# Three steps' weight sums are made early and kept in DRAM, and two more steps of the last round go by sums

## The chip, the cores and the metric

One core of one Trainium2 chip runs the whole kernel. Five engines work side by side, each through its own list of instructions in order: TensorE (PE, with its weight loads as PEld) multiplies, VectorE (DVE) and ScalarE (ACT) do elementwise work, GpSimd (POOL) does a little of it and issues some transfers, SyncE (SP) issues nearly all others. The metric is the time of one execution on the device in microseconds (us), as the median of several runs.

## The reference

The reference is one layer of a streaming encoder for 256 tokens of width 2048, all in float32: a gated linear attention, then an MLP with squared ReLU, each behind an RMSNorm and with a residual, and a last RMSNorm.

```python
h = x
h = h + gla_mixer(rmsnorm(h, gla_norm), w_in, w_gate_up, b_gate, o_norm, w_out)   # q, k, v, r and a gate out of w_in
h = h + (relu(rmsnorm(h, mlp_norm) @ w_up) ** 2) @ w_down                          # 2048 -> 8192 -> 2048
return rmsnorm(h, final_norm)
```

Nearly all time goes into products of the 256 tokens with float32 weights, which come from DRAM once each.

## The kernel before

**Products in parts.** A float32 number is used as the sum of two: `hi`, a rounded copy that ScalarE makes (`copy_hi`), and `lo`, what is left, a subtraction on VectorE. A product is then three matmuls, hi by hi, hi by lo and lo by hi. A weight tile of 512 KB thus goes: SP loads it into a `raw` tile (six of them and one more, in turn), ScalarE makes hi, VectorE makes lo, each into one of five slots (`slots()`), and TensorE multiplies. ScalarE and VectorE run ahead of TensorE by as many steps as there are slots free.

**Products by sums.** For the down product of the MLP (and parts of w_out) a step takes a pair of 128 weight rows by 512 columns, as a 2 by 2 grid of blocks. A plain step is 8 block products of 3 matmuls, 24 in all. A step "by sums" (Strassen's way in Winograd's form) forms sums of the activations' blocks (`form_sums`) and of the weight's blocks (`weight_sums`) and makes 7 block products, 21 matmuls. It costs VectorE and ScalarE more: first hi and lo of three quarters of the raw tile, whose first quarter is meanwhile turned into a sum by an accumulating DMA of POOL, then two instructions of `weight_sums` in place in the raw tile, then hi and lo of the whole tile again (`of_sums`). TensorE correspondingly has two parts, 9 matmuls on the raw tile and later 12 on the sums; they add into four PSUM banks, P16, B32, P57 and BX4.

**The order of the work.** First the mixer: `natural` and `turned` stream the columns of w_in (v, k, q, then the rest of v, then r); small work between steps is queued in `side` and done by `pump`, one item per step. In the order of the trace the second half of v is multiplied from about 140 us (line 554). Then w_out, then the MLP in eight rounds of 1024 hidden units: `up` makes the round's activations, `down` adds the round's part of the result. Up steps run 18 ahead of down steps and interleave with them. `down` goes through passes (m, g), round m and column group g, four steps kp = 0 to 3 each. When the up steps have ended, the last ten down steps run alone: (6, 0) from kp 2, (7, 0) and (7, 1). Column groups 2 and 3 of the last round come after these, as eight plain steps of another shape (line 1229 on), which use two further tiles, `room` and `hf`, in the place of the turned activations `hth` and `htl` (tags Ah and Al).

**What goes by sums.** `by_sums(m, g, kp)` (line 850) says it: all steps of rounds 0 to 5, most of round 6, and in round 7 only (0, 2), (0, 3) and (1, 2), written (g, kp).

**Banks between passes.** When a pass of a new column group begins, the banks of the old group are saved to SBUF and new ones are filled from it, both by ScalarE: `settle(k)` does the saving of bank k (`sums<-acc` or `h<-acc` in the profile), `begin(k, g)` the filling (`acc<-sums` or `acc<-h`). Where they stand among the steps hangs on `first`, the first step of the pass that goes by sums: in a pass that runs alone P16 is saved and filled at `kp == first`, P57 at the step after, B32 and BX4 are saved at that step too (line 1162). All of these copies go through `copy_end`, and a later `copy_hi` is put behind the last of them in ScalarE's list (`last_end`).

Of the kernel before, what the change touches and what calls it, by code (L numbers as in the profile page):

```python
# [46 lines left out]
G = 1024  # L47
GT = 512
# [13 lines left out]
MR = 2 * GT  # L62
ROUNDS = HID // MR
# [5 lines left out]
def tile_gla_mlp(ctx, tc, x, xt, cols, w_vg, w_in, w_gate, w_out, w_up, w_down, final_norm, out):  # L69
    nc = tc.nc  # L70

    const = ctx.enter_context(tc.tile_pool(name="const", bufs=1))
    big = ctx.enter_context(tc.tile_pool(name="big", bufs=2))
# [2 lines left out]
    tmp = ctx.enter_context(tc.tile_pool(name="tmp", bufs=2))  # L76
    st = ctx.enter_context(tc.tile_pool(name="st", bufs=3))
    psum = ctx.enter_context(tc.tile_pool(name="psum", bufs=1, space=bass.MemoryType.PSUM))

    acc_free, aux_free = deque(range(6)), deque([6, 7])  # L80

# [9 lines left out]
        return psum_bank(aux_free[-1], "aux")  # L91


    side = deque()

    def pump(n=1):

        with tc.issue_after(last_hi[0].ins), tc.issue_after(last_lo[0].ins):
            for _ in range(n):
                if side:  # L100
                    side.popleft()()

    def flush():
        while side:
# [5 lines left out]
    last_load, last_hi, last_lo, last_sum, last_end = [None], [None], [None], [None], [None]  # L110
# [9 lines left out]
    def slots():  # L120
        return [wpool.tile([P, SLOT], F32R, tag=i, name=i) for i in ("hi", "lo")]
# [56 lines left out]
    def natural(row, source, n, cuts, pumps=1, ahead=None, order=range(KT)):  # L178

        acc = acc_banks(NT * len(cuts))  # L180
        acc = [acc[t * len(cuts) : (t + 1) * len(cuts)] for t in range(NT)]
        for step, kt in enumerate(order):
            wh, wl = weights(source(kt), n, ahead and ahead(kt))
            terms = lambda t: [(row(kt, t)[x], (wh, wl)[y]) for x, y in ((0, 0), (0, 1), (1, 0))]
            if ahead and step == 0:
                for c, (lo, hi) in enumerate(cuts):
                    for i in (0, 2, 1):
                        for t in range(NT):
                            s, w = terms(t)[i]
# [16 lines left out]
    def turned(row, w, c0, even=(0,), acc=None):  # L206

        acc = acc or acc_banks(GT // P // 2)
        for kp in range(KT // 2):
            wh, wl = pair_of(w, kp, c0, even)  # L210
            for i in range(2):
                kt = 2 * kp + i
                ah, al = row(kt)
                for j in range(GT // P):
                    s = slice(j * P, (j + 1) * P)
                    o = acc[j // 2][:, j % 2 * T : (j % 2 + 1) * T]
                    for n, (u, m) in enumerate(((wh, ah), (wh, al), (wl, ah))):

                        nc.tensor.matmul(  # L219
                            o, u[:, i, s], m, start=kt == 0 and n == 0 and j % 2 == 0,  # L220
                            stop=kt == KT - 1 and n == 2, skip_group_check=True,
                        )
                if kt < KT - 1:
                    pump()
        return acc

    HALF = [(0, 512), (512, 1024)]
# [323 lines left out]
    side.extend([nothing] * 4 + [lambda: two_scores(0), nothing, lambda: two_scores(2)])  # L551


    acc = natural(row_x, rows(w_in, 3 * KEYW), G, HALF, order=even_at(9, 11))
    flush()
    for t in range(NT):
# [46 lines left out]
    def weight_sums(u):  # L603
        nc.vector.tensor_tensor(u[:, 2], u[:, 0], u[:, 2], op=ALU.subtract)  # L604
        return nc.vector.tensor_tensor(u[:, 1::2], u[:, 1::2], u[:, 2:3].to_broadcast([P, 2, T]), op=ALU.subtract)  # L605

    FORMED = (0, 1, 7)
    in_forms = lambda a: a.rearrange("p (f s) -> p f s", f=8)
# [241 lines left out]
    def by_sums(m, g, kp):  # L850

        if m == ROUNDS - 1:
            return (g, kp) in ((0, 2), (0, 3), (1, 2))
        return m < ROUNDS - 2 or g != order_of(m)[-1] or kp == 1


# [174 lines left out]
    def down(passes):  # L1031
# [3 lines left out]

        ahead = pending = None
        quick = False
        units = 0
        for n, (m, g) in enumerate(passes):
            fresh = not n or passes[n - 1][1] != g  # L1040
# [11 lines left out]
            for kp in range(KP):  # L1052
                last = ends and kp == KP - 1
                alone = units + LEAD >= UPS
                by_parts = by_sums(m, g, kp)

                def products(n, these, w, banks=banks, last=last):

# [11 lines left out]
                raw = raw_tile()[:, : 2 * GT]  # L1070
                c0 = m * MR + 2 * kp * P
                src = w_down[c0 : c0 + 2 * P, g * GT : (g + 1) * GT].rearrange("(i p) c -> p i c", p=P)
                if by_parts:
                    for i in range(2):
                        last_load[0] = nc.sync.dma_start(out=raw[:, i * GT : (i + 1) * GT], in_=src[:, i])

                    nc.gpsimd.dma_start(out=raw[:, :T], in_=src[:, 0, T:], accum_op=ALU.add)  # L1077
                else:
                    last_load[0] = nc.sync.dma_start(out=raw.rearrange("p (i c) -> p i c", i=2), in_=src)
# [13 lines left out]
                if by_parts:  # L1093
                    these = (P16, 0, at(A11), block(1)), (B32, T, at(A12), block(3)), (B32, 0, at(S4), block(2))
                    u = raw.rearrange("p (f s) -> p f s", f=4)

                    with tc.issue_after(last_lo[0].ins):
                        last_sum[0] = weight_sums(u).ins
                else:
                    these = [  # L1100
                        (k, 0, at(f[i]), block(2 * i, 2))
                        for i in range(2) for k, f in ((B32, (A11, A12)), (BX4, (A21, A22)))
                    ]
# [10 lines left out]

                ahead_of = passes[n + 1] if last and n + 1 < len(passes) else None

                def of_sums(u=raw, products=products, at=at, kp=kp, banks=banks, quick=fresh and quick, g=g, then=ahead_of):


                    nonlocal ahead  # L1120
                    to = slots()

                    if quick and kp < 2:
                        settle((B32, P16)[kp])
                        if kp == 0:
                            banks[P57] = begin(P57, g)
                    if then and by_sums(*then, 0):
                        ahead = {k: begin(k, then[1]) for k in (B32, P16)}
                    for a in range(2):
                        copy_hi(*(x.rearrange("p (f s) -> p f s", f=4)[:, a::2] for x in (to[0][:, :G], u)))  # L1130
                    if quick and kp == 0:
                        settle(P57)
                        banks[BX4] = begin(BX4, g)
                    elif quick and kp == 1:
                        settle(BX4)
                    with tc.issue_after(last_lo[0].ins):
                        last_lo[0] = nc.vector.tensor_tensor(to[1][:, :G], u, to[0][:, :G].bitcast(F32), op=ALU.subtract)  # L1137
                    early = (P57, 0, at(S1), block(0)), (P16, T, at(S2), block(2))
                    late = (P57, T, at(S3), block(1)), (BX4, T, at(A22), block(3))
                    products(0, early, to)  # L1140
                    yield
                    products(0, late, to)
                    products(1, (*early, *late), to)

                if by_parts:
                    if alone:

                        pending = of_sums()
                    else:
                        rest = of_sums()  # L1150
                        next(rest)
# [167 lines left out]
```

## Time and profile before

| | us |
|---|---|
| median of 3 runs (lowest to highest) | 1044.37 (1044.07 to 1044.48) |
| the profiled execution, its own time | 1043.33 |
| its span, first to last instruction | 1041.5 |
| busy in the span: TensorE, VectorE, ScalarE, POOL | 1033.2, 865.3, 736.9, 119.5 |
| share of the chain of waits that is TensorE's | 99% |

A row of a group shows line, engine, operation, output and inputs, shape and count, then busy time in us, mean time of one in ns, and the engine's idle time before it with what ended most of it. A row of the timeline shows start and duration in us, then the same, and in brackets the idle time before and its releaser; equal instructions in a row are merged (x8). Times of the timeline count from the start of the span. A row of the stretches shows a window, its length, the busy time of each engine (PE, PEld, DVE, ACT, POOL) with the number of instructions, the granted clock, the busy share of the DMA engines and what they moved in GB/s. A row of the issues shows the transfer, the engine whose queue it is, the count, the size of one and the median time in us from issue to landing. TensorE's matmuls overlap, so the steps between starts tell its pace, not the durations.

### The profile page before, as it was taken

What the parts mean: (1) busy time and instruction counts of PE and PEld (TensorE: products, weight loads), DVE (VectorE), ACT (ScalarE), POOL (GpSimd) and SP (SyncE); (2) the same over time, 40 slices, a digit from 0 to 9 for tenths busy, and PEclk for the clock granted to TensorE, in tenths of its full rate; (3) what the DMA queues carried; (4) which work ended last, traced back from release to release, by engine and by line L of the source; (5) the groups of instructions that cost most, each with busy time, mean ns of one, the idle gap of its engine ahead of it and who ended that gap; (6) DMA issues with size and microseconds to landing.
All of it is one profiled execution on the core that took longest, in us unless ns stands there. A gap on an engine that the chain in (4) does not pass through costs nothing.

```text
span 1041.5 us, 23180 instructions
## 1 busy us (share of the span) xinstructions
PE 1033.2 (99%) x9058; PEld 1032.8 (99%) x9058; DVE 865.3 (83%) x1171; ACT 736.9 (71%) x1088; POOL 119.5 (11%) x163
## 2 busy tenths in 40 slices
PE   9999999999999999999999999999999999999997
PEld 9999999999999999999999999999999999999997
DVE  6668654657599876989999999999999999999887
ACT  7685544546477665677778788778778778778685
POOL 0000000010111101111111121111111121111100
PEclk9999999999999999999999999999999999999999
DMA  9957664655667687678887887887888888887772
GB/s 341 338 164 220 189 199 144 181 145 180 194 182 210 206 263 197 175 207 239 224 249 226 230 233 227 233 243 214 253 227 225 245 228 228 237 233 219 234 243 86
DMA packets 119453, 226.79 MB, mean 218 GB/s; under 512 B 10752, under 2 KB 27904, under 8 KB 119216
## 3 DMA queue, kind: packets, MB, share of 16 engines
q1 hardware_dynamic: 100768, 207.46, 63.2%
q0 software_dynamic: 17856, 16.26, 10.3%
q10 hardware_dynamic: 720, 1.60, 0.4%
q8 instruction: 71, 1.16, 0.4%
q14 instruction: 38, 0.31, 0.1%
HBM read 223.17 MB, written 2.10 MB: 216 GB/s over the span
## 4 chain that ended last, share of the span: by engine, by line
PE 99%; issue 0%; ACT 0%; DVE 0%; POOLq 0%; POOL 0%; DVEq 0%
PE up L867 33%; PE acc L867 28%; PE acc L176 19%; PE acc L725 8%; PE acc L219 6%; PE aux L219 2%; PE aux L176 1%; PE aux L627 1%; PE aux L523 1%; PE aux L252 0%; ACT sqf L1206 0%; PE acc L424 0%; DVE hf L1278 0%; POOLq L1315 0%; POOL rf L358 0%
## 5 line engine op out<-in xcount | busy, mean ns | idle before, releaser
L118 ACT CAST hi<-raw 128x512 fp32r<-128x512 f32 (+4 forms) x634 | 512.0, 834 | 234.8 <-PE acc L176 69.0
L131 DVE TENSOR_TENSOR lo<-raw,hi 128x768 fp32r<-128x768 f32 (+3 forms) x226 | 238.0, 1057 | 100.1 <-ACT hi L118 97.4
L867 PE MATMUL acc<-hi,act 128*128 128x256 f32 x1696 | 247.7, 276 | 0.0
L867 PE MATMUL up<-hh,hi 128*128 128x256 f32 x1024 | 238.7, 276 | 0.0
L867 PE MATMUL up<-hl,hi 128*128 128x256 f32 x1024 | 238.7, 276 | 0.0
L165 DVE TENSOR_TENSOR lo<-raw,hi 128x1024 fp32r<-128x1024 f32 x160 | 194.7, 1219 | 28.3 <-ACT hi L118 26.3
L867 PEld LDWEIGHTS acc<-hi,act 128*128 128x128 f32 x1696 | 217.6, 188 | 0.0
L867 PEld LDWEIGHTS up<-hl,hi 128*128 128x128 f32 x1024 | 192.2, 188 | 0.0
L867 PEld LDWEIGHTS up<-hh,hi 128*128 128x128 f32 x1024 | 192.2, 188 | 0.0
L1077 POOL DMA_DIRECT2D raw<-in_w_down x112 | 97.1, 867 | 516.1 <-DMA raw<-in_w_down 231.0
L1137 DVE TENSOR_TENSOR lo<-raw,hi 128x1024 fp32r<-128x1024 f32 x112 | 136.4, 1218 | 1.1 <-ACT hi L118 1.1
L867 PE MATMUL up<-hh,lo 128*128 128x256 f32 x1024 | 137.0, 276 | 0.0
L867 PE MATMUL acc<-lo,act 128*128 128x256 f32 x848 | 133.8, 276 | 0.0
L867 PEld LDWEIGHTS up<-hh,lo 128*128 128x128 f32 x1024 | 125.7, 188 | 0.0
L867 PEld LDWEIGHTS acc<-lo,act 128*128 128x128 f32 x848 | 113.4, 188 | 0.0
L176 PE MATMUL acc<-hi,xA 128*128 128x256 f32 (+1 forms) x736 | 105.6, 278 | 0.0
L176 PEld LDWEIGHTS acc<-hi,xA 128*128 128x128 f32 x736 | 94.4, 188 | 0.0
L605 DVE TENSOR_TENSOR raw<-raw 128x512 f32<-128x512 f32 x124 | 85.6, 690 | 3.2
L176 PE MATMUL acc<-lo,xA 128*128 128x256 f32 (+1 forms) x368 | 61.5, 278 | 0.0
L604 DVE TENSOR_TENSOR raw<-raw 128x256 f32<-128x256 f32 x124 | 52.4, 423 | 2.9
L176 PEld LDWEIGHTS acc<-lo,xA 128*128 128x128 f32 x368 | 50.8, 188 | 0.2 <-DVE lo L131 0.2
L219 PE MATMUL acc<-xA,hi 128*128 128x256 f32 x288 | 49.2, 276 | 0.0
(181 smaller groups left out, 1220.0 us busy)
## 6 DMA issues: line engine op xcount, KB each, us to landing
raw<-in_w_up SPq DMA_DIRECT2D x128, 512.0 KB, 4.6
raw<-in_w_down SPq DMA_DIRECT2D x224, 256.0 KB, 4.3
raw<-in_w_in SPq DMA_DIRECT2D x80, 512.0 KB, 3.8
raw<-in_w_down POOLq DMA_DIRECT2D x112, 128.0 KB, 5.0
raw<-in_w_out SPq DMA_DIRECT2D x20, 512.0 KB, 4.9
raw<-in_w_down SPq DMA_DIRECT2D x16, 512.0 KB, 5.0
raw<-in_w_vg SPq DMA_DIRECT2D x14, 520.0 KB, 8.1
raw<-in_w_out SPq DMA_DIRECT2D x24, 256.0 KB, 3.5
```

Source lines behind the costliest of these rows:

```text
L118: last_hi[0] = nc.scalar.copy(to, raw)
L131: last_lo[0] = nc.vector.tensor_tensor(lo[:, s], raw[:, s], hi[:, s].bitcast(F32), op=ALU.subtract)
L165: last_lo[0] = nc.vector.tensor_tensor(to[1], dst, to[0].bitcast(F32), op=ALU.subtract)
L176: nc.tensor.matmul(o[:, m], x, w[:, m], start=first and c == 0, stop=last, skip_group_check=True)
L219: nc.tensor.matmul(o, u[:, i, s], m, start=kt == 0 and n == 0 and j % 2 == 0, stop=kt == KT - 1 and n == 2, skip_group_check=True,)
L523: nc.tensor.matmul(o, kab[:, k[0], c0 + c, k[1] : k[1] + P], q(qt[:, c0 + c]), start=c == 0, stop=c == 1)
L604: nc.vector.tensor_tensor(u[:, 2], u[:, 0], u[:, 2], op=ALU.subtract)
L605: return nc.vector.tensor_tensor(u[:, 1::2], u[:, 1::2], u[:, 2:3].to_broadcast([P, 2, T]), op=ALU.subtract)
L725: newest[0] = nc.tensor.matmul(bank[:, o + d : o + d + T], x, w[:, d : d + T], start=bank in sums_banks and bank.name not in begun, stop=l ...
L867: newest[0] = nc.tensor.matmul(o, x, w, start=first, stop=last, skip_group_check=True).ins
L1077: nc.gpsimd.dma_start(out=raw[:, :T], in_=src[:, 0, T:], accum_op=ALU.add)
L1137: last_lo[0] = nc.vector.tensor_tensor(to[1][:, :G], u, to[0][:, :G].bitcast(F32), op=ALU.subtract)
```

## The change

In the last round five steps instead of three go by sums: (0, 2), (0, 3), (1, 1), (1, 2), (1, 3). The weight sums of the last three, those of pass (7, 1), are no longer made in `down`. They are made in the mixer: `make_sums` loads the weight tile with SP into a raw tile, VectorE forms all sums in it (three instructions), ScalarE and VectorE make hi and lo in a pair of the slots, and two DMAs of POOL store them, 512 KB each, in DRAM tiles. Each of the three tiles is two jobs and an empty one; `pump` does one job per step, so they go with the first nine steps of the second half of v. In the order in which the built kernel's instructions stand, these loads come among that pass's loads in SP's list, and the six stores are next to each other in POOL's list.

In `down` these three steps load three quarters of their raw tile (in two transfers), and hi and lo of the sums (two transfers of 512 KB) into `pre` tiles, which take the place of `hth` and `htl`; SP's list has the sums of kp 3 ahead of those of kp 1 and 2. The accumulating DMA, `weight_sums` and the second hi and lo go away there. TensorE does the 9 matmuls of kp 1, the 9 of kp 2, the 12 of kp 1, the 9 of kp 3 and then the 12 of kp 2 and of kp 3. With (1, 1) by sums `first` of pass (7, 1) is 1 and no longer 2, so that the savings and fillings of the banks stand one step earlier. Before pass (7, 1) TensorE's list is the same in both kernels. The activations of (7, kp 1) now need `form_sums`, and their parts are made over the full width.

```diff
+    dram = ctx.enter_context(tc.tile_pool(name="dram", bufs=1, space=bass.MemoryType.DRAM))
...
-    side = deque()
+    side, jobs = deque(), deque()
...
                 if side:
                     side.popleft()()
+            if jobs:
+                jobs.popleft()()
...
+    MADE_DOWN = ((1, 1), (1, 2), (1, 3))
+    made = {}
+
+    def make_sums(key, src):
+
+        made[key] = dram.tile([2, P, G], F32, tag=f"made{len(made)}", name="made")
+        raw, to = [], []
+
+        def high():
+            raw.append(raw_tile()[:, :G])
+            with tc.issue_after(last_load[0].ins):
+                last_load[0] = nc.sync.dma_start(out=raw[0].rearrange("p (i c) -> p i c", i=2), in_=src)
+            u = raw[0].rearrange("p (f s) -> p f s", f=4)
+            nc.vector.tensor_tensor(u[:, 0], u[:, 0], u[:, 1], op=ALU.add)
+            weight_sums(u)
+            to.extend(slots())
+            nc.scalar.copy(to[0][:, :G], raw[0])
+            nc.gpsimd.dma_start(out=made[key][0], in_=to[0][:, :G].bitcast(F32))
+
+        def low():
+            nc.vector.tensor_tensor(to[1][:, :G], raw[0], to[0][:, :G].bitcast(F32), op=ALU.subtract)
+            nc.gpsimd.dma_start(out=made[key][1], in_=to[1][:, :G].bitcast(F32))
+
+        return high, low
...
+        for high, low in todo:
+            jobs.extend([high, low, lambda: None])
...
+    make_all()
     acc = natural(row_x, rows(w_in, 3 * KEYW), G, HALF, order=even_at(9, 11))
...
         if m == ROUNDS - 1:
-            return (g, kp) in ((0, 2), (0, 3), (1, 2))
+            return (g, kp) in ((0, 2), (0, 3), (1, 1), (1, 2), (1, 3))
...
+                ready = made.get((m, g, kp))
...
-                if by_parts:
+                if ready is not None:
+                    last_load[0] = nc.sync.dma_start(out=raw[:, T:GT], in_=src[:, 0, T:])
+                    last_load[0] = nc.sync.dma_start(out=raw[:, GT:], in_=src[:, 1])
+                    if not rooms:
+                        for i in "hl":
+                            rooms.extend(big.tile([P, 2, 2, G], F32R, tag="A" + i, name="pre", bufs=1).rearrange("p b i c -> b p i c"))
+                    ready_in = rooms.pop(0)
+                    for i in range(2):
+                        last_load[0] = nc.sync.dma_start(out=ready_in[:, i].bitcast(F32), in_=ready[i])
+                    ready = [ready_in[:, i] for i in range(2)]
+                elif by_parts:
...
-                    with tc.issue_after(last_lo[0].ins):
-                        last_sum[0] = weight_sums(u).ins
+                    if not ready:
+                        with tc.issue_after(last_lo[0].ins):
+                            last_sum[0] = weight_sums(u).ins
...
-                    to = slots()
+                    copied = not to
+                    to = to or slots()
...
-                    for a in range(2):
+                    for a in range(2 * copied):
                         copy_hi(*(x.rearrange("p (f s) -> p f s", f=4)[:, a::2] for x in (to[0][:, :G], u)))
...
-                    with tc.issue_after(last_lo[0].ins):
-                        last_lo[0] = nc.vector.tensor_tensor(to[1][:, :G], u, to[0][:, :G].bitcast(F32), op=ALU.subtract)
+                    if copied:
+                        with tc.issue_after(last_lo[0].ins):
+                            last_lo[0] = nc.vector.tensor_tensor(to[1][:, :G], u, to[0][:, :G].bitcast(F32), op=ALU.subtract)
...
                         pending = of_sums()
+                        if last and n + 1 == len(passes):
+                            for _ in pending:
+                                pass
```

More of the change, by code (lines that the diff above doesn't have):

```diff
@@ L225, in turned, with weight_sums, make_all @@
         return acc
+    def weight_sums(u):
+        nc.vector.tensor_tensor(u[:, 2], u[:, 0], u[:, 2], op=ALU.subtract)
+        return nc.vector.tensor_tensor(u[:, 1::2], u[:, 1::2], u[:, 2:3].to_broadcast([P, 2, T]), op=ALU.subtract)
+    MADE_OUT = ()
+    MADE_DOWN = ((1, 1), (1, 2), (1, 3))
[17 more added lines that the diff above has]
+        return high, low
+    def make_all():
+        pair = lambda w, c0, g: w[c0 : c0 + 2 * P, g * GT : (g + 1) * GT].rearrange("(i p) c -> p i c", p=P)
+        todo = [make_sums((None, g, kp), pair(w_out, 2 * kp * P, g)) for g, kp in MADE_OUT]
+        todo += [make_sums((ROUNDS - 1, g, kp), pair(w_down, (ROUNDS - 1) * MR + 2 * kp * P, g)) for g, kp in MADE_DOWN]
+        for high, low in todo:
+            jobs.extend([high, low, lambda: None])
     HALF = [(0, 512), (512, 1024)]
@@ L601, in form_sums @@
         tt(f[:, S4], f[:, A12], f[:, S2], ALU.subtract)
-    def weight_sums(u):
-        nc.vector.tensor_tensor(u[:, 2], u[:, 0], u[:, 2], op=ALU.subtract)
-        return nc.vector.tensor_tensor(u[:, 1::2], u[:, 1::2], u[:, 2:3].to_broadcast([P, 2, T]), op=ALU.subtract)
     FORMED = (0, 1, 7)
@@ L1037, in down @@
         quick = False
+        rooms = []
         units = 0
@@ L1115, in down, with of_sums @@
                 ahead_of = passes[n + 1] if last and n + 1 < len(passes) else None
-                def of_sums(u=raw, products=products, at=at, kp=kp, banks=banks, quick=fresh and quick, g=g, then=ahead_of):
+                def of_sums(u=raw, products=products, at=at, kp=kp, banks=banks, quick=fresh and quick, g=g, then=ahead_of, to=ready):
                     nonlocal ahead
-                    to = slots()
+                    copied = not to
+                    to = to or slots()
                     if quick and kp < 2:
```

## The prediction, made before the changed kernel ran

> **What bounds the kernel now.** I read the page first, then the chain of waits, then the timelines of TensorE, ScalarE, VectorE and SyncE in the two stretches that the change touches.
>
> ```profile
> span 1041.5 us, 23180 instructions
> PE 1033.2 (99%) x9058; PEld 1032.8 (99%) x9058; DVE 865.3 (83%) x1171; ACT 736.9 (71%) x1088; POOL 119.5 (11%) x163
> ...
> GB/s 341 338 164 220 189 199 144 181 145 180 194 182 210 206 263 197 175 207 239 224 249 226 230 233 227 233 243 214 253 227 225 245 228 228 237 233 219 234 243 86
> ...
> PE 99%; issue 0%; ACT 0%; DVE 0%; POOLq 0%; POOL 0%; DVEq 0%
> ```
>
> TensorE is the chain from end to end; the other engines matter only where they make it wait. So a change is worth the matmuls that it removes, less the waits that it adds. The end of the last round, as TensorE runs it:
>
> ```profile
> 1003.15 1.07 PE L867 MATMUL acc<-hi,act 128*128 128x256 f32 x8
> 1004.06 0.62 PE L867 MATMUL acc<-lo,act 128*128 128x256 f32 x4
> 1004.51 1.98 PE L867 MATMUL acc<-hi,act 128*128 128x256 f32 x16
> 1006.32 1.07 PE L867 MATMUL acc<-lo,act 128*128 128x256 f32 x8
> 1007.23 0.84 PE L867 MATMUL acc<-hi,act 128*128 128x256 f32 x6
> 1007.91 0.50 PE L867 MATMUL acc<-lo,act 128*128 128x256 f32 x3
> ...
> 1012.33 0.96 PE L176 MATMUL acc<-hi,act 128*128 128x256 f32 x7
> ```
>
> A plain step is 24 matmuls (16 hi, 8 lo), from 1004.51 to 1007.23: 2.72 us, 0.113 each. A step by sums is 21, in two parts: 9 on the raw tile (1007.23), later 12 on its sums (1003.15 shows the 12 of pass (7,0), kp 3). In 1003.15 to 1012.33 nothing waits.
>
> **The matmuls saved.** In pass (7,1) kp 1 and kp 3 go from 24 to 21: 6 x 0.113 = 0.68 us less. That is all that the change can give TensorE; the order before pass (7,1)'s second step stays the same.
>
> **The new wait at 1004.5.** ScalarE and VectorE in that stretch:
>
> ```profile
> 999.75 2.31 ACT L118 CAST hi<-raw 128x512 fp32r<-128x512 f32 x3
> 1004.48 0.59 ACT L994 COPY sums<-acc 128x512 f32<-128x512 f32 x1 [2.42 <-PE acc L867]
> 1004.96 0.60 ACT L994 COPY acc<-sums 128x512 f32<-128x512 f32 x1
> 1005.48 1.05 ACT L118 CAST hi<-raw 128x1024 fp32r<-128x1024 f32 x1
> ...
> 1009.51 1.08 ACT L994 COPY h<-acc 128x512 f32<-128x512 f32 x2
> 1010.47 1.07 ACT L118 CAST hi<-raw 128x1024 fp32r<-128x1024 f32 x1
> ```
> ```profile
> L118 ACT CAST hi<-raw 128x768 fp32r<-128x768 f32 x124 | 103.1, 832 | 6.5 <-PE up L867 2.1 <-ACT some L780 1.7 <-PE acc L176 1.7
> L131 DVE TENSOR_TENSOR lo<-raw,hi 128x768 fp32r<-128x768 f32 x124 | 118.1, 953 | 25.5 <-ACT hi L118 23.8 <-PE up L867 1.4 <-DMA raw<-in_w_down 0.2
> ```
>
> At 1004.48 ScalarE saves bank P16 of the pass just ended and at 1004.96 fills P16 of pass (7,1); the 2.42 us before are a wait for TensorE's last matmul into the old P16. Now this costs nothing: `settle(P16)` stands at kp 2, behind two casts, and TensorE has 24 plain matmuls to run. In the changed kernel the first step by sums is kp 1, so the pair stands at kp 1, ahead of the cast of kp 2, and TensorE has only kp 1's 9 to run, of which the last 3 write P16. The pair can't start sooner: it waits for the same matmul. Queued behind it on ScalarE: the cast of kp 2, P57's pair, two copies h<-acc (now at kp 2 too), the cast of kp 3. Worked with the rows' durations; release and restart come from the one wait of this kind that the trace has:
>
> ```profile
> 10.19 1.24 DVE L131 TENSOR_TENSOR lo<-raw,hi 128x1040 fp32r<-128x1040 f32 x1 [1.06 <-ACT hi L118]
> ...
> 11.49 0.41 PEld L176 LDWEIGHTS acc<-lo,xA 128*128 128x128 f32 x3 [0.23 <-DVE lo L131]
> 11.49 0.62 PE L176 MATMUL acc<-lo,xA 128*128 128x256 f32 x3
> ```
>
> VectorE ended at 11.43, TensorE started at 11.49: release 0.06. Three matmuls took 0.62 against 0.50 at 1007.91: restart 0.12.
>
> - 1004.51 plus 6 matmuls = 1005.19. P16 is filled at 1005.56, released at 1005.62: wait 0.43.
> - Three matmuls and a restart: 1006.08. Cast of kp 2: 1005.48 + 0.83 = 1006.31, released 1006.37: wait 0.29.
> - Six: 1007.17. VectorE's lo of kp 2: 1006.34 + 0.95 = 1007.29, released 1007.35: wait 0.18.
> - Three, then kp 1's 12 from the stored sums (P57 filled at about 1007.3, in time): 1009.17. The copies h<-acc take ScalarE from 1007.2 to 1008.2, the cast of kp 3 to 1009.0, in time. Six: 1009.85. Lo of kp 3: 1009.03 + 0.95, released 1010.04: wait 0.19.
> - Three, 12 of kp 2, 12 of kp 3: 1013.22.
>
> The 1012.33 row thus moves to 1013.22. Waits 1.09 and four restarts 0.48 make 1.57; less 0.68, that is +0.89 us. Ends: no wait at all, -0.68, if the copies ended sooner than their rows say; or each wait longer by a ScalarE copy of 0.6 that slips ahead, +1.5. I take the replay, since every term has its row a few us away.
>
> The rest runs later by the same 0.9: from 1009.94 ScalarE's casts for the final steps come some 0.5 us sooner than now (1010.47), so nothing more waits there. The output's tail behind the last matmul is not touched.
>
> **The loads of the sums.** They go into the room of the turned activations, free when the last up matmul has run:
>
> ```profile
> 983.77 0.28 PE L867 MATMUL up<-hl,hi 128*128 128x256 f32 x1
> ...
> 984.34 1.07 PE L867 MATMUL up<-hh,lo 128*128 128x256 f32 x8
> ```
> ```profile
> 981.31 0.80 SPq L1075 DMA_DIRECT2D raw<-in_w_down  x2
> 983.07 0.38 SPq L1079 DMA_DIRECT2D raw<-in_w_down  x1
> 988.85 0.81 SPq L1075 DMA_DIRECT2D raw<-in_w_down  x2
> 991.24 0.38 SPq L1079 DMA_DIRECT2D raw<-in_w_down  x1
> 993.36 19.79 SPq L168 DMA_DIRECT2D raw<-in_w_down  x8
> ```
> ```profile
> 983.00:1006.00 23.00, 23.00 (x206) 23.00 (x205) 19.52 (x27) 15.19 (x21) 1.72 (x2) 1.00 0.82 243
> ```
> ```profile
> fb<-in_final_norm ACTq DMA_DIRECT2D x1, 1024.0 KB, 6.7
> ```
>
> SyncE has 12 issues for kp 1 to 3 where it had 4; 8 x 0.40 = 3.2 us of a queue that is mostly free. Kp 3's sums stand first and wait for the lo half's room until 984.1 (SyncE would have issued kp 1's raw at 983.07); kp 1's raw follows at 984.9 instead, kp 1's and kp 2's sums at 985.4 to 987. Behind them stand kp 2's raw (988.85, held by a raw tile anyway), kp 3's, and the final steps' eight. Three MiB of sums come in, 0.5 MiB of raw loads goes: +2.6 MB. Needed first: kp 2's raw at 1005.5, behind 3.75 MiB of SyncE's own and the 1.2 MB that ScalarE's and POOL's queues load there (the gain row above and one sum of 128 KB): 5.1 MB in 21.7 us, 235 GB/s; this stretch moves 243, the page's first slice 341. At 341 it lands 7 us early, so I take 0; the other end is in the rivals.
>
> **VectorE before the end.** Kp 1's activation forms of round 7 now need sums: three more adds and a full-width subtract, where VectorE has no idle time:
>
> ```profile
> 962.92 0.96 DVE L131 TENSOR_TENSOR lo<-raw,hi 128x768 fp32r<-128x768 f32 x1 [0.16 <-ACT hi L118]
> ...
> 972.32 1.22 DVE L1137 TENSOR_TENSOR lo<-raw,hi 128x1024 fp32r<-128x1024 f32 x1
> ```
> ```profile
> 975.08 0.62 PE L867 MATMUL acc<-lo,act 128*128 128x256 f32 x4
> 986.61 1.08 DVE L972 TENSOR_TENSOR work<-work 128x128 f32<-128x128 f32 x3
> ```
>
> The adds are 1.08 at most, the wider subtract 0.5, less the 0.16 idle: 1.4 at worst. The tightest lo ends at 973.54 and is used at 975.08: 1.54 of cover. Cost between 0 and, if the cover is gone, 1.4; I take 0, since the 1.54 is read from rows of this stretch.
>
> **The mixer.** Each of the three jobs adds a load, four VectorE instructions (that engine is busy 17 of the 35 us below), a cast of 1.05 and two stores of 512 KB through POOL, and holds one pair of the five hi/lo slots until they land.
>
> ```profile
> 128.84 1.06 ACT L118 CAST hi<-raw 128x1024 fp32r<-128x1024 f32 x1 [1.67 <-PE acc L219]
> ```
> ```profile
> 139.64 0.62 PE L176 MATMUL acc<-hi,xA 128*128 128x256 f32 x4
> ```
> ```profile
> 130.00:165.00 35.00, 35.00 (x310) 35.00 (x309) 16.95 (x19) 14.89 (x19) 0.00 (x0) 1.00 0.65 195
> ```
> ```profile
> raw<-in_w_vg SPq DMA_DIRECT2D x14, 520.0 KB, 8.1
> ...
> out<-hf SPq DMA_DIRECT2D x5, 256.0 KB, 2.6
> ```
>
> The cast of the pass's first step ends 9.7 us before its use (129.90 to 139.64). A job takes one slot, one step of 2.72: 7.0 left. Stores: 2.6 us for half the bytes here; 8.1 for a transfer of this size with the queues full. The first job's copy falls one step later, to about 131.6, and its second store to about 138; the slot's next user is needed at 150.5, so a store has some 12 us. Bandwidth: 4.7 MB more in nine steps (24.5 us) is 193 GB/s on 195, 47 above the 341 seen: 3.4 us of lag, inside 7.0. POOL is idle there (x0), so its queue holds nobody up. Cost 0.
>
> By the Trainium skill ("DMA: Bandwidth & Descriptors", Anatomy of one DMA) a transfer tells of its end only when its last byte is confirmed in the target, with HBM the slowest target. By that page's fit a store would be 3.2 us, an estimate that leaves the sum alone; its warning is the third rival.
>
> **Sum.** 1043.33 (the profiled execution, 1.04 under the median of the runs) + 0.89 = 1044.2; on the median of 1044.37 it is 1045.3, +0.09%. A measurement of this kernel can tell about 0.2%, 2.1 us, from no change.
>
> **Rivals.**
> - *The saving comes through.* TensorE loses no time at 1005 and the end is 0.68 sooner: 1043.7. For it: every number of the waits is below 0.5 us, and the trace of before has no wait at all after the start. Against it: the copy at 1004.48 is bound to a TensorE matmul that doesn't move. Chance 0.2.
> - *The loaded sums come late* (the other side). Decides below 235 GB/s between 984 and 1005.5: at 200, near the mixer's row, 5.1 MB take 25.5 us, 3.8 late, and with the 0.9 that is 1049.1. For it: 82% of the queues' time is used in that stretch already. Against: 341 at the start. Chance 0.1.
>  By the Trainium skill ("TensorE: Matmul & The Clock Gate", What's actually happening) an idle window of about 3.4 us would also halve the clock for a while; no run here shows one.
> - *A store holds its slot* longer than 12 us, and the cast behind it comes late: three jobs, each one step of 2.7: up to +8, 1053 with the rest; at 14 us, 3 x 2 = +6, 1051. For it: loads and stores above 341 GB/s together. Against: 2.6 and 8.1. Chance 0.07.
> - *VectorE's 1.4 us before 973 break through* on top of the forecast: 1046.7, inside the range. For it: no idle time there. Against: the 1.54. Chance 0.05, taken from the forecast's.
>
> **How the numbers follow.** The forecast's case has 0.55 (1044.6 to 1046.2), VectorE's 0.05, the clean saving 0.2, late loads 0.1, slots 0.07, and 0.03 for a gain that I don't see. Faster by over 0.2% would need three times the matmuls removed: 0.03. Slower by over 0.2% is the two late cases, less their mild ends: 0.14. Within: 0.83. The range runs from the clean saving less the runs' spread, 1043.4, to the mild late cases, 1047.0.
>
> **What will show it.** Right: TensorE pauses of 0.2 to 0.5 us at about 1005, 1006, 1007 and 1010, the first two released by ScalarE, the others by VectorE, and nothing else on the chain; the final steps begin about 0.9 later than 1012.33. Wrong: no pause there; a wait of TensorE for the loaded sums; a pause between 140 and 190; or a late lo near 975.

## The result

| | median, us | lowest to highest | runs |
|---|---|---|---|
| before | 1043.82 | 1043.21 to 1044.48 | 20 |
| changed | 1045.55 | 1045.14 to 1046.02 | 20 |

The ratio is 1.0016, with a 95% interval of 1.0010 to 1.0022: 1.73 us slower. The forecast was a change of less than 0.2%, with +0.89 us on this kernel's time. The sign and the places were right, the size was about half of what came. That the forecast time, 1045.3 us, lies only 0.25 us from the measured 1045.55 is in part luck: it stood on a median of three runs, 1044.37, which is 0.55 us above that of the twenty, and this hides most of the 0.84 us that the size lacks.

The page of the changed kernel; the columns are those of the page before:

```profile
span 1043.3 us, 23219 instructions
PE 1034.7 (99%) x9052; PEld 1033.6 (99%) x9052; DVE 871.3 (84%) x1183; ACT 738.6 (71%) x1089; POOL 120.8 (12%) x168
...
PE 98%; issue 1%; ACT 0%; DVE 0%; POOLq 0%; POOL 0%; DVEq 0%
```

TensorE has six matmuls fewer (9052 against 9058) and is busy 1.5 us longer. The timeline of TensorE in the changed kernel, at the end of the last round:

```profile
1004.58 0.62 PE L905 MATMUL acc<-hi,act 128*128 128x256 f32 x4
1005.04 0.39 PE L905 MATMUL acc<-lo,act 128*128 128x256 f32 x2
1005.69 0.50 PE L905 MATMUL acc<-hi,act 128*128 128x256 f32 x2 [0.26 <-ACT acc L1032]
1006.03 0.28 PE L905 MATMUL acc<-lo,act 128*128 128x256 f32 x1
1006.45 0.98 PE L905 MATMUL acc<-hi,act 128*128 128x256 f32 x6
1007.44 0.63 PE L905 MATMUL acc<-lo,act 128*128 128x256 f32 x3
1007.91 1.57 PE L905 MATMUL acc<-pre,act 128*128 128x256 f32 x12
1009.32 0.87 PE L905 MATMUL acc<-hi,act 128*128 128x256 f32 x6
1010.15 0.62 PE L905 MATMUL acc<-lo,act 128*128 128x256 f32 x3
1010.61 2.99 PE L905 MATMUL acc<-pre,act 128*128 128x256 f32 x24
1013.44 0.99 PE L179 MATMUL acc<-hi,act 128*128 128x256 f32 x7
...
1035.35 0.87 PE L179 MATMUL acc<-room,act 128*128 128x256 f32 x6
```

Two things are to be seen. The forecast's four pauses are there: the starts leave gaps ahead of 1005.69, 1006.45, 1007.44 and 1010.15. And the matmuls behind them are slower. The last 24 of the pass take from 1010.61 to 1013.44, 2.83 us or 0.118 each, where the kernel before has 0.113. The last row of the same timeline before:

```profile
1033.41 0.84 PE L176 MATMUL acc<-room,act 128*128 128x256 f32 x6
```

So the delay is 1013.44 - 1012.33 = 1.11 us at the first of the final steps and 1.94 us at the last six matmuls (0.1 of either is the start of the execution), though no matmul waits in between.

The trace's list of matmuls, one start each, gives an exact account. "Pace" is the time from the start of one matmul to the start of the next (128x128 stationary tile, 256 columns). I count from the 81st matmul, which lies behind the last stall of the start (12.5 to 13.5 us, different in every execution), to the last matmul.

| | 81st to last matmul, us | against before |
|---|---|---|
| before | 1021.44 | |
| changed, two executions | 1023.29, 1023.29 | +1.85 |

The 1.85 come apart as follows: six matmuls fewer, -0.68; four pauses, +1.49 over the pace of 113.3 ns; and 240 matmuls behind the first pause at 117.8 instead of 113.3 ns, +1.08 (a pause here is the gap and the longer interval behind it, less two paces). The sum is 1.89, 0.04 above what the two ends give. From 60 to 1005 us the two kernels have the same pace, and from the 81st to the 8781st matmul (1002.6 us) they differ by 0.03 us.

### The profile page after: what moved, and what is told of

It is laid out like the page before. It is cut to its first block, busy times and chain, and to the rows that moved or that the text cites. A ratio compares the mean times of both kernels' runs of the same rounds, so it can differ in the third digit from the quotient of the medians.

```text
span 1043.3 us, 23219 instructions
## 1 busy us (share of the span) xinstructions
PE 1034.7 (99%) x9052; PEld 1033.6 (99%) x9052; DVE 871.3 (84%) x1183; ACT 738.6 (71%) x1089; POOL 120.8 (12%) x168
## 4 chain that ended last, share of the span: by engine, by line
PE 98%; issue 1%; ACT 0%; DVE 0%; POOLq 0%; POOL 0%; DVEq 0%; ACTq 0%
PE up L905 33%; PE acc L905 28%; PE acc L179 18%; PE acc L763 8%; PE acc L222 6%; PE aux L222 2%; PE aux L179 1%; PE aux L665 1%; PE aux L564 1%; PE aux L293 0%; ACT sqf L1262 0%; PE acc L465 0%; ACT hi L121 0%; DVE hf L1334 0%; POOLq L1371 0%
## 5 line engine op out<-in xcount | busy, mean ns | idle before, releaser
L905 PE MATMUL acc<-hi,act 128*128 128x256 f32 x1668 | 244.8, 276 | 0.4 <-ACT acc L1032 0.3
L905 PEld LDWEIGHTS acc<-hi,act 128*128 128x128 f32 x1668 | 214.5, 188 | 0.8 <-ACT acc L1032 0.5
```

The lines of the kernel that those rows point to most:

```text
L905: newest[0] = nc.tensor.matmul(o, x, w, start=first, stop=last, skip_group_check=True).ins
```

## The experiments

Theory P was formed on these two traces: a pause puts TensorE into a slower pace, which holds until stationary tiles on another offset are loaded. Almost all stationary tiles here begin 64 bytes off a multiple of 128 (`OFF` is 48 floats). A few steps of earlier stages have tiles on a multiple of 128, as the one that `up` runs at about 610 and 979 us. In both traces the pace is 117 to 118 ns from the start to the first such step at about 59 us (but for eleven matmuls of the changed kernel at about 12 us, to which the last experiment comes back), and 113.3 behind it.

**No pauses.** The banks of the last pass are filled without first saving those of the pass before; two other banks are free by then.

```diff
+                elif fresh and kp == first and m == ROUNDS - 1 and g == 1:
+                    banks.update({k: begin(k, g) for k in (P16, P57)})
                 elif fresh and kp == first:
                     settle(P16)
                     banks[P16] = begin(P16, g)
+                elif fresh and kp == KP - 1 and m == ROUNDS - 1 and g == 1:
+                    settle(P16, P57, B32, BX4)
...
-                if fresh and kp == first + alone and not quick:
+                if fresh and kp == first + alone and not quick and (m, g) != (ROUNDS - 1, 1):
```

> The changed kernel, but in the last pass of the down product the two banks of sums (P16, P57) are filled without first emptying the pass before: two other banks are free by then; the four banks of the pass before are emptied three steps later. Theory P (two paces): the 1.73 us that the change costs are the four pauses of TensorE at about 1005 to 1008 us (1.6 us with their restarts), and a slower pace of every matmul behind the first pause (117.8 ns from start to start, 113.3 before it: some 250 matmuls by 4.45 ns, 1.1 us), less the six matmuls saved (0.68 us). Without the pauses both go: 113.3 ns to the end, no gap over 0.13 us behind 1000 us, and the time is 0.6 to 0.8 us below the kernel before (ratio 0.9993). Rival L (the late pace comes from the loads of the sums, or from matmuls on tiles that a load filled): no pauses, but 117.8 ns from about 1005 us on, so 0.3 to 0.5 us above the kernel before. Rival N (the pauses come elsewhere, as a cast of ScalarE is late next): pauses of 0.3 us or more remain at 1006 to 1010 us and the time is between the two kernels.

Measured: 1042.68 us against 1043.94 for the kernel before on the same chip, ratio 0.999 (0.9981 to 0.9999). It is the fastest of the three kernels. (One of its eleven executions took 1044.64 us; no trace of that one was kept.) ScalarE's timeline in this run, and under it TensorE's:

```profile
1001.17 1.10 ACT L1032 COPY acc<-sums 128x512 f32<-128x512 f32 x2
1002.21 1.57 ACT L121 CAST hi<-raw 128x768 fp32r<-128x768 f32 x2
1004.62 1.08 ACT L1032 COPY sums<-acc 128x512 f32<-128x512 f32 x2 [0.85 <-PE acc L905]
```
```profile
1004.65 0.84 PE L905 MATMUL acc<-hi,act 128*128 128x256 f32 x6
1005.33 0.50 PE L905 MATMUL acc<-lo,act 128*128 128x256 f32 x3
1005.67 0.84 PE L905 MATMUL acc<-hi,act 128*128 128x256 f32 x6
1006.35 0.50 PE L905 MATMUL acc<-lo,act 128*128 128x256 f32 x3
...
1009.07 2.88 PE L905 MATMUL acc<-pre,act 128*128 128x256 f32 x24
1011.79 0.73 PE L179 MATMUL acc<-hi,act 128*128 128x256 f32 x5
```

The two banks are filled at 1001.17, and both casts are done at 1003.78, before ScalarE stops for TensorE at all. TensorE runs through: the same 24 matmuls on loaded sums take 1009.07 to 1011.79, 2.72 us, so neither those tiles nor their loads make the pace slow. From the 81st to the last matmul it is 1020.76 us, 0.68 below before: exactly the six matmuls. Rivals L and N fall. The median fell by 1.26, more than 0.68; 0.2 of it lies behind the last matmul (7.31 us to the end, before 7.53), and the rest is within the interval and stays open.

**The offset.** The changed kernel, pauses and all, with the first final step's upper stationary tiles read from a copy. In one run the copy begins on a multiple of 128 bytes, in the other 64 bytes off it; TensorE has the same instructions in the same order.

```diff
+                    if (m, g, kp) == (ROUNDS - 1, 1, KP - 1):
+                        moved.append(mid.tile([P, 4 * T], F32R, tag="ee", name="moved")[:, :T].rearrange("p (i s) -> p i s", i=2))
+                        for i, x in enumerate(stationary(m, 0, A11)):
+                            nc.vector.tensor_copy(moved[0][:, i], x.bitcast(F32))
...
+        if kt == t == 0:
+            a = [moved[0][:, i] for i in range(2)]
```

The second run differs from the first in one slice:

```diff
-name="moved")[:, :T]
+name="moved")[:, OFF : OFF + T]
```

> The changed kernel with all its pauses, but the two stationary tiles of the first final step's upper half are read from a copy that begins on another offset (a multiple of 128 bytes; the others begin 64 bytes off that). VectorE makes the copy well ahead. In the traces of both kernels the pace of 117 to 118 ns that follows the stalls of the start ends at the steps whose stationary tiles have such an offset. Theory P: 117.8 ns from the first pause at 1005 us up to these 12 matmuls, about 120 ns in them, and 113.3 ns behind them to the end: some 200 matmuls by 4.45 ns, so 0.8 to 1.0 us below the changed kernel, 0.7 to 0.9 us above the kernel before. Rival L (the pace is the tail's own, or the loads'): no change from the changed kernel, 1.6 to 1.8 us above the kernel before.

> The run with the copied stationary tiles again, but the copy begins 192 bytes further on, 64 bytes off a multiple of 128 as all the other stationary tiles of the last steps do. The instructions of TensorE and their order are the same. Theory O (the offset ends the slower pace): the 117.8 ns stay to the end, 1.5 to 1.9 us above the kernel before, as the changed kernel. Rival K (any change to another tile, or the copy itself, ends it): 113.3 ns behind the twelve matmuls, 0.7 to 0.9 us above the kernel before, as the run with the copy on the other offset.

Measured: 1044.77 us with the copy on the multiple of 128 (kernel before 1043.94, ratio 1.0007, 0.9999 to 1.0016), and 1045.43 with the copy on the usual offset (kernel before 1043.89, ratio 1.0015, 1.0006 to 1.0024). The changed kernel was run again as well:

> The changed kernel as it is, for its time beside the others of this call: 1.5 to 2.0 us above the kernel before, and four pauses at 1005 to 1008 us again, with 117.8 ns behind them.

It gave 1045.50 us (kernel before 1043.89). A view of stretches shows how many matmuls lie in the same 14 us near the end, at a granted clock of 1.00 in each row (start and end, length, busy time with counts of PE, PEld, DVE, ACT, POOL, then clock, DMA share, GB/s). First the copy on the multiple of 128, then the copy on the usual offset:

```profile
1017.00:1031.00 14.00, 14.00 (x126) 14.00 (x125) 12.36 (x20) 8.68 (x19) 0.00 (x0) 1.00 0.01 1
```
```profile
1017.00:1031.00 14.00, 14.00 (x121) 14.00 (x120) 12.29 (x19) 8.34 (x18) 0.00 (x0) 1.00 0.00 0
```

The kernel before has 126 there too, the changed kernel 122. In the list of matmuls the first run has 118 ns up to the twelve moved matmuls (the last starts at 1015.16 us) and 113.3 behind, 1022.53 us from the 81st to the last; the second has 117.8 to the end and 1023.29, the changed kernel's number. So here the offset ends the slower pace, and neither the copy nor another tile does. Restoring the pace was worth 0.76 us by the list, 0.78 by the medians.

**A pause elsewhere.** The kernel before, with one pause added where nothing of the change is near. VectorE copies a bank of an up product between two halves of a step. In a first pair of runs this was the product's first bank:

```diff
+            if i == 0 and (c0, kp) == (2 * MR + 0 * GT, 3):
+                seen = tmp.tile([P, 512], F32, tag="t512", name="seen", bufs=1)
+                nc.vector.tensor_copy(seen[:, :512], acc[0])
```

> The kernel before with one pause put into the middle: in the fourth step of the third round's first up product VectorE copies one bank of that product (128x512) into scratch between the step's first and second half, and TensorE, which goes on in that bank, must wait for it: a pause of some 0.3 to 0.6 us at about 450 us, far from the last round, with no load of a made sum in the kernel. Nothing uses the copy. The next step with stationary tiles on the other offset runs at about 610 us, and another at about 979 us. Theory P: 113.3 ns before the pause, 117.8 ns behind it up to 610 us (some 1400 matmuls by 4.45 ns: 6.2 us) and 113.3 ns from there: 6 to 7 us above the kernel before. Rival Q (the pause costs its own length alone): 113.3 ns on both sides, 0.3 to 0.8 us above the kernel before.

> The same pause, in the sixth step of the fourth round's first up product, right ahead of the step at about 610 us whose stationary tiles have the other offset. Theory P: 117.8 ns for the matmuls between the pause and that step only (fewer than 60, 0.3 us), so 0.4 to 1.0 us above the kernel before, and some 5 to 6 us below the run with the early pause. Rival S (a pause sets the slower pace for good, and the offset has no part in it): 117.8 ns from 610 us to the end, some 3700 matmuls by 4.45 ns, 16 us above the kernel before. Rival Q: the same as with the early pause, 0.3 to 0.8 us above, and no 117.8 ns anywhere behind 61 us.

Neither theory was tested: 1043.97 and 1043.73 us against 1043.82, and 1021.44 us of matmuls in both, as before. The matmuls of the other bank were put in front, and TensorE did not wait. What it shows is that 0.69 us more of VectorE cost nothing at these two places. The second pair of runs copies the second bank (`acc[1]`), which holds the last matmul of the half, in (round 1, second product, step 3) and in (round 3, first product, step 5):

> The kernel before with one pause put into its middle, this time on the bank that the next block of matmuls cannot go around: in the fourth step of the second round's second up product VectorE copies the second bank of that product (128x512) into scratch between the step's halves. The copy takes 0.69 us by the run before, and 0.45 us of matmuls stand between: a pause of 0.2 to 0.5 us at some 460 to 490 us. Nothing uses the copy. Theory P: 113.3 ns from start to start before it, 117.8 ns behind it up to the step with the other offset at 610 us (some 1100 matmuls or more by 4.45 ns: about 5 us), 113.3 ns from there: 4.5 to 7 us above the kernel before. Rival Q (a pause costs its own length, and the slower pace has another cause): 113.3 ns on both sides, 0.2 to 0.6 us above.

> The same pause in the sixth step of the fourth round's first up product, at about 606 us, right ahead of the step at 610 us with the other offset. Theory P: 117.8 ns for the fewer than 60 matmuls up to that step alone: 0.3 to 0.8 us above the kernel before, and 113.3 ns from there to the end. Rival S (the slower pace stays, and the offset has no part in ending it): 117.8 ns from 606 us to the end, some 3700 matmuls, 16 us above. Rival Q: 0.2 to 0.6 us above, no 117.8 ns behind 61 us.

Measured: 1049.81 us for the early pause (before 1043.89, ratio 1.0048, 1.0033 to 1.0063) and 1044.78 for the late one (ratio 1.0007, 0.9998 to 1.0016). The early pause in TensorE's timeline:

```profile
473.47 0.28 PE L867 MATMUL up<-hl,hi 128*128 128x256 f32 x1
474.07 0.39 PE L867 MATMUL up<-hh,hi 128*128 128x256 f32 x1 [0.33 <-DVE seen L923]
474.30 0.28 PE L867 MATMUL up<-hl,hi 128*128 128x256 f32 x1
```

And stretches ahead of the step at about 610 to 620 us and behind it, for the early pause, then for the late one:

```profile
420.00:460.00 40.00, 40.00 (x356) 40.00 (x355) 35.30 (x47) 27.78 (x41) 5.17 (x6) 1.00 0.70 197
480.00:520.00 40.00, 40.00 (x342) 40.00 (x342) 38.12 (x50) 29.00 (x42) 6.07 (x7) 1.00 0.84 234
560.00:600.00 40.00, 40.00 (x342) 40.00 (x341) 38.08 (x51) 30.94 (x45) 6.93 (x8) 1.00 0.84 234
620.00:660.00 40.00, 40.00 (x356) 40.00 (x355) 37.70 (x51) 33.82 (x51) 6.05 (x7) 1.00 0.82 225
```
```profile
560.00:600.00 40.00, 40.00 (x356) 40.00 (x355) 38.85 (x51) 30.88 (x45) 6.07 (x7) 1.00 0.83 236
620.00:660.00 40.00, 40.00 (x355) 40.00 (x354) 38.37 (x50) 34.32 (x53) 6.93 (x8) 1.00 0.84 236
```

One pause that itself costs 0.6 us (0.60 from 473.47 to 474.07 and 0.23 to the next start, less two paces) takes 14 of 356 matmuls from every 40 us behind it, up to the step on the other offset; there the full number is back. From the pause to the step on the other offset the list has some 1200 matmuls at 117.8 ns in this run, some 40 with the late pause, and 6.01 and 0.77 us more from the 81st to the last matmul. Theory P's 4.5 to 7 us came; its 0.3 to 0.8 came by the list, while the medians have 0.89. Rivals Q and S fall. Of the six runs with the early pause five took 1049.61 to 1050.13 us and one 1044.36. No trace of that one was kept; its time is that of the pause without the slower pace, so a pause seems not to set the slower pace every time.

**Two steps made, and the mixer alone.** The first has (1, 1) as a plain step again, the second makes the sums in the mixer and reads none of them.

```diff
-    MADE_DOWN = ((1, 1), (1, 2), (1, 3))
+    MADE_DOWN = ((1, 2), (1, 3))
...
-            return (g, kp) in ((0, 2), (0, 3), (1, 1), (1, 2), (1, 3))
+            return (g, kp) in ((0, 2), (0, 3), (1, 2), (1, 3))
```

```diff
-            return (g, kp) in ((0, 2), (0, 3), (1, 1), (1, 2), (1, 3))
+            return (g, kp) in ((0, 2), (0, 3), (1, 2))
...
-                ready = made.get((m, g, kp))
+                ready = None
```

> Only two of the three steps are made in the mixer, and (1, 1) stays a plain step: four of the last round's eight steps go by sums, as against three before and five in the changed kernel, and the first of the last pass's steps by sums is its third, as in the kernel before. TensorE then has the 24 matmuls of the second plain step ahead of the filling of the first bank of sums. Theory P: no pause, 113.3 ns to the end, three matmuls fewer: 0.3 us below the kernel before (0.1 to 0.5). Rival L: the loads and tiles of the made sums are still there, 117.8 ns from about 1007 us: 0.5 to 0.8 us above the kernel before. Rival N (any second step by sums in that pass makes ScalarE late): a pause of 0.2 to 0.5 us and the slower pace behind it, 0.8 to 1.3 us above the kernel before.

> The kernel before with the changed kernel's work in the mixer alone: the three jobs load, sum, split and store as in the changed kernel, but no later step reads what they made, and three steps of the last round go by sums as before. The forecast's steps 4 and 5: the mixer's part costs nothing, so within 0.1 us of the kernel before (ratio 1.0000 +- 0.0002). Rival M (the mixer's loads, casts or stores delay something): up to 1.0 us above, and TensorE's starts from the mixer's stage on are later than in the kernel before.

Measured: 1043.74 and 1043.71 us against 1043.94 (0.9999, 0.9990 to 1.0008; 0.9997, 0.9988 to 1.0006). The list decides where the medians can't: 1021.10 us with two steps made, 0.34 below before, three matmuls and no pause; 1021.44 with the mixer's part alone, no change to 0.01 us.

**The slower pace of the start.** The run without pauses, and in the kernel's first product one tile step on the other offset:

```diff
+    def one_even_x(kt, t):
+        return (row_x if kt == EVEN[1] else plain_x)(kt, t)
+
-    acc = natural(plain_x, rows(w_vg, 0, WMAX), WMAX, cuts, ahead=input_tile)
+    acc = natural(one_even_x, rows(w_vg, 0, WMAX), WMAX, cuts, ahead=input_tile)
```

> The run that fills the banks first (the fastest so far), and in the first product of the kernel the seventh tile step, at about 22 us, takes its upper half's stationary tiles from the copy with the other offset, which is made there already and used by later stages. Theory P: the slower pace that follows the stalls of the start (117.8 ns up to about 59 us in all traces so far) ends at about 24 us: some 290 matmuls by 4.45 ns, so 1.0 to 1.4 us below the run that fills the banks first, about 2.3 us below the kernel before. Rival T (the pace of the first 59 us has to do with the stage itself: its loads, its 272-wide matmuls): no change from that run.

Measured: 1042.82 us, against 1042.68 without it. Theory P's 1.0 to 1.4 us did not come; it is rival T's no gain. TensorE's timeline behind the new tiles (`xe_gt`):

```profile
23.21 0.52 PE L179 MATMUL acc<-hi,xe_gt 128*128 128x256 f32 x3
23.57 0.50 PE L179 MATMUL acc<-hi,xA 128*128 128x256 f32 x3
23.90 0.50 PE L179 MATMUL acc<-lo,xA 128*128 128x256 f32 x3
24.25 0.50 PE L179 MATMUL acc<-hi,xA 128*128 128x256 f32 x3
...
25.09 0.29 PE L179 MATMUL acc<-lo,xA 128*128 128x272 f32 x1
...
25.70 0.51 PE L179 MATMUL acc<-lo,xA 128*128 128x256 f32 x3
```

The nine matmuls behind the new tiles do run at 113.3 ns (23.57 to 24.59). Then this stage's six matmuls of 272 columns come, and behind them it is 117 to 118 again. So in this stage the pace is lost anew in each step. That the 272 columns do it is the likely reading; a kernel without them was not run.

The same stretch of the kept traces shows that theory P is too simple. Between 10 and 12.2 us TensorE waits for its first tiles in some executions, always with 117 to 118 ns ahead of the first such stall and all stationary tiles on the usual offset. Behind the stall the kernel before goes on at 118. In five traces (both of the changed kernel, both with the copied tiles, and the late pause) eleven matmuls at 113 follow, up to the next 272 columns. In the run with the new tiles one stall brings 113 and the next, 1.3 us later, brings 118 back. So a pause can end the slower pace too, and the offset isn't the only thing that does. In the other direction the traces agree: all seven pauses that were met at 113 ns (four at the end of the last round, the two added ones, and this last one) left 118 behind them. What decides it isn't shown.

## Why the prediction was right or wrong

- *The matmuls saved, -0.68.* Right: the run without pauses shows exactly 0.68 in the list.
- *The new wait at 1004.5.* Right, in places, releasers and sizes. The pause with its restart, forecast against measured (the gap and the one behind it, less two paces of 113.3 ns): 0.55 and 0.53; 0.41 and 0.42; 0.30 and 0.30; 0.31 and 0.24. The sum is 1.49 against 1.57. ScalarE and VectorE, the changed kernel:

```profile
1004.56 0.59 ACT L1032 COPY sums<-acc 128x512 f32<-128x512 f32 x1 [3.36 <-PE acc L905]
1005.04 0.59 ACT L1032 COPY acc<-sums 128x512 f32<-128x512 f32 x1
1005.56 0.83 ACT L121 CAST hi<-raw 128x768 fp32r<-128x768 f32 x1
```
```profile
1006.43 0.96 DVE L134 TENSOR_TENSOR lo<-raw,hi 128x768 fp32r<-128x768 f32 x1 [3.48 <-ACT hi L121]
1009.14 0.96 DVE L134 TENSOR_TENSOR lo<-raw,hi 128x768 fp32r<-128x768 f32 x1 [1.75 <-ACT hi L121]
```

 The pair of copies, the cast queued behind it (done at 1006.39, TensorE's start 1006.45) and the two lo (1007.39 and 1007.44, 1010.10 and 1010.15) release the four starts, as the replay had it.
- *"The rest runs later by the same 0.9."* This is the step that failed. It took 0.113 us for every matmul behind the pauses. They ran at 0.1178, 240 of them, and that is the 1.08 us that the sum lacks, 0.2 of it ahead of 1013.44. A hint was in the trace of before, next to the row that the restart of 0.12 was taken from, and I read the restart and not the row behind it:

```profile
11.95 0.52 PE L176 MATMUL acc<-hi,xA 128*128 128x256 f32 x3
```

 Three matmuls in 0.52 there, in 0.50 at 1007.91: there is a second pace. That a pause brings it this trace could not tell, since the matmuls ahead of that stall have it too (0.118 each from 10.48 to 11.07). The changed kernel's trace even has the faster pace for the same three matmuls behind the same stall:

```profile
12.08 0.50 PE L179 MATMUL acc<-hi,xA 128*128 128x256 f32 x3
```

 That a pause late in the kernel leaves the slower pace is shown by the runs alone: without the pauses it doesn't come, with one pause put into the kernel before it does.
- *The loads of the sums, 0.* Right. SyncE issued them where forecast, and no matmul waited for them:

```profile
984.15 0.83 SPq L1121 DMA_DIRECT2D pre<-made  x2
985.08 0.42 SPq L1114 DMA_DIRECT2D raw<-in_w_down  x1
985.55 0.58 SPq L1115 DMA_DIRECT2D raw<-in_w_down  x1
986.22 2.05 SPq L1121 DMA_DIRECT2D pre<-made  x4
```
```profile
983.00:1006.00 23.00, 22.74 (x200) 22.54 (x200) 17.99 (x24) 14.03 (x20) 1.18 (x2) 1.00 1.01 372
```

 The stretch moved 372 GB/s; the rival of late loads needed less than 235.
- *VectorE before the end, 0.* Right. The tightest lo ends at 973.22 + 1.22 = 974.44 and is used at 975.15: 0.71 of the 1.54 us of cover is left.

```profile
973.22 1.22 DVE L1190 TENSOR_TENSOR lo<-raw,hi 128x1024 fp32r<-128x1024 f32 x1
```
```profile
975.15 0.62 PE L905 MATMUL acc<-lo,act 128*128 128x256 f32 x4
```

- *The mixer, 0.* Right, by the run that made the sums and read none. The stores land in 4.1 and 7.3 us, where the slot had 12:

```profile
made<-hi POOLq DMA_DIRECT2D x3, 512.0 KB, 4.1
made<-lo POOLq DMA_DIRECT2D x3, 512.0 KB, 7.3
```

- *"The output's tail is not touched."* Nearly: 7.35 us from the last matmul's start to the end, 7.53 before.
- *The rival of the clean saving.* It fell here because the save of the old bank stands ahead of the filling of the new one on ScalarE. Against it the forecast said that the copy at 1004.48 can't move. Of the pair only the save is bound to TensorE's matmul; the filling could go to another bank, and then the rival's time came and more.

## What to carry to other kernels

Price a pause on the engine that bounds the kernel by what follows it, too: compare in the trace the spacing of the instructions ahead of a known stall and behind it, and not only the stall and the restart. Where the trace has no stall like the one forecast, put one in and measure it. In a bank that is saved and filled again, only the save has to wait for the last user; if another bank is free, fill that one first and save later, off the path. When totals differ by less than the runs scatter, a list of the instructions from one fixed point to another shows shares of 0.1 us that medians don't.

## What the runs showed of the hardware

A stream of matmuls (128x128 stationary, 256 columns, a weight load for each) has two steady paces at the same granted clock of 1.00: 113.3 and 117.8 ns from start to start, 4%. A pause of up to 0.5 us can change the one for the other. All seven pauses that the traces have at the faster pace ended in the slower one, though by its time one untraced run of six with the early pause kept the faster. Of the pauses at the slower pace those of the last round kept it (three in each of four traces), while those of the start mostly ended it (six traces of seven). Once set, the slower pace held over a thousand matmuls, through both up and down products. Twelve matmuls whose stationary tiles begin 64 bytes off the usual ones (116 to 121 ns each themselves) bring the faster pace back.

By the Trainium skill ("TensorE: Matmul & The Clock Gate", Back-to-back issue gap) an isolated gap is N / 2.4 + 2.5 ns, by estimate 109.2 for 256 columns, and a stream of loads and matmuls is set by both together; the traces have 113.3 at best. The same page's clock gate (What's actually happening) halves the clock after an idle window of about 3.4 us; here the pauses last 0.6 us at most, the clock stayed at 1.00, and the loss was 4%, so the gate as the page has it isn't the cause.

What happens inside stays open: the runs show that a pause late in the kernel is followed by the slower pace and that the offset ends it, not why, nor why a pause at the start can do the reverse.
